# A 32-row rest of turned attention scores written by ScalarE and VectorE in place of transfers, and first-stage rows laid down by parity

## The chip, the cores and the metric

The kernel runs on one core of a Trainium2 chip. The metric is the device time of one execution in microseconds (us), the median of several runs. The engines are TensorE (PE, its weight loads PEld), VectorE (DVE), ScalarE (ACT), GpSimd (POOL) and SyncE (SP), which here only issues transfers.

## What is computed

One layer of a hybrid encoder block over 512 tokens of width 2048, in float32: a normalised and modulated input, one wide projection, two token mixers that read it (a dilated sliding-window attention with 16 heads of 64, and a gated linear attention with 4 heads), gates, an output projection, a residual and a final norm. The change lies in the first projection and in the attention, of which this is the core:

```python
for window, dilation in ((128, 1), (512, 4), (2048, 16)):
    s = einsum(q, keys at +-dilation*j) * E ** -0.5 + bias   # j up to 64, masked
    p = exp(s - max(s));  den = sum(p)
    o_p = (p / den) @ v                                      # and log-sum-exp lse_p
att = sum over patterns of softmax(lse)[p] * o_p
```

The kernel merges the three patterns into one softmax: a pair of positions that several patterns allow has the logarithm of their number added to its bias, and a pair that none allows is masked.

## The kernel before

**Numbers and products.** A float32 product is made of three products of two halves, `hi` (the rounded operand) and `lo` (what is left): hi*hi, lo*hi, hi*lo, lines 229, 230 and 231. So every operand is written twice, `hi` by ScalarE as a copy into a rounding type, and `lo` by VectorE as a subtraction. Weights come in by transfer as `raw_*` tiles and are split so at lines 493 (ScalarE) and 477 (VectorE).

**First stage.** Stage `a` (PSUM tiles `sta`, 16 steps `k`) multiplies the scaled input h by the attention's value weights; stage `b` (`stb`) makes the first queries and keys. `u_high` and `u_low` (lines 525 to 530) write h from x, 512 tokens a step. The values are wanted with even tokens ahead of odd ones. Before, h keeps the order of the tokens here, and stage `a` takes its stationary operand from h with `TOKENS`, four slices of 128 tokens with step two. Ahead of stage `b` h is written once more, in the order of the tokens.

**Attention.** It runs in the background of four projections, called units: `qk2`, `qk4`, `qk6` (which make the queries and keys of later heads) and `gk`. Each unit is 64 ticks of three matmuls of 512 columns; the attention of four heads is spread over it, as a list of items with places in the unit that come from `ATT_AT`. A head has four tiles `i` of 128 queries, and a tile has:

- `score(h, i)`: two matmuls of 416 columns into PSUM tile `s` (lines 817, 818); VectorE adds the bias from tile `g` and takes the least (825); ScalarE takes the exponential and its sum in place in tile `p` (829); VectorE the reciprocal (832); GpSimd scales the tile (836; ScalarE for the last two, 834).
- `turn(h, i)`, two scores later: three transposes of 128 columns into `t` (851), then ScalarE's `hi` (855) and VectorE's `lo` (856) into `pt`, one of two tiles that hold the turned scores of a pair of query tiles.
- `rest(h, e)`, with every second turn: 416 columns are three times 128 and 32 more. The 32 more of each of the two tiles of the pair are transposed into `r` (865), rounded and subtracted into a helper tile of 32 rows (867, 868), and sent by two transfers (871, on SP's queue) to their rows of `pt`: rows 96 to 127 for one half, rows 0 to 31 for the other.
- `values(h, e)`, once a pair: eight matmuls of 256 columns (880) over the four chunks of `pt` in the order 1, 2, 3, 0. Chunks 1 and 2 hold no row of the rest. Then 883 (ScalarE) and 887 (VectorE) write the head's output.

Beside each score VectorE does a piece of side work: token sums (1189 and after, 0.7 us) or bias sums of 1024 columns (959, 328).

**Order.** TensorE's order is the program's: per step x the list holds `score(x)`, `values` of the pair whose second tile was scored five steps ago, `turn(x - 2)`. The other engines' order is chosen by the scheduler of the language, which follows the dependences. PSUM has a ring of three buffers for `s`, `t` and `o`, and of five for the unit's four sums and `r`. SP issues all in order: weights, bias rows `g`, the rests, and the duplicates of queries (762, 765) and keys (774) across the two halves of the partitions, which `qk_evict` makes at the end of each unit.

Of the kernel before, what the change touches and what calls it, by code (L numbers as in the profile page):

```python
# [10 lines left out]
F32 = mybir.dt.float32  # L11
# [7 lines left out]
P = 128  # L19
# [90 lines left out]
ATT_AT = (0.17, 0.8, 0.04, 0.05, 0.02, 0.1)  # L110
# [80 lines left out]
def block_kernel(ctx: ExitStack, tc: tile.TileContext, a: dict):  # L191
# [332 lines left out]

    def u_high(k):
        act(h_hi[:, k, :], x_of(k), AF.Copy, scale=scale[:, k:k + 1])

    def u_low(k):
        stt(h_lo[:, k, :], x_of(k), scale[:, k:k + 1], h_hi[:, k, :].bitcast(F32),
            op0=ALU.mult, op1=ALU.subtract)  # L530
# [41 lines left out]
    def first_products(z, e):  # L572
# [3 lines left out]
        for i in range(4):  # L576
            j, t = 4 * z + i, TOKENS[i]
# [4 lines left out]
    def products(st, k, j):  # L582
# [3 lines left out]
        if st == "a":  # L586
            t, c = TOKENS[j % 4], slice(j // 4 * 512, j // 4 * 512 + 512)
# [164 lines left out]
    def qk_evict(p, psq, psk):  # L752
# [3 lines left out]
        for j in range(2):  # L756
            own = slice(64 * j, 64 * j + 64)
            oth = slice(64 - 64 * j, 128 - 64 * j)
            qh, ql = T2(f"qh{p}{j}", F32R), T2(f"ql{p}{j}", F32R)
# [6 lines left out]
            stacks[2 * p + j] = [qh, ql, None, own]  # L766
        for j in range(2):
            own = slice(64 * j, 64 * j + 64)
            oth = slice(64 - 64 * j, 128 - 64 * j)
            ks = key_tile(2 * p + j)  # L770
            src = psk[own].rearrange("p (c a) -> p a c", a=2)
            act(by_parity(ks, own), src, AF.Copy)
            tt(by_parity(ks, oth), src, by_parity(ks.bitcast(F32), own), op=ALU.subtract)
            nc.sync.dma_start(ks[:, 512:768].bitcast(F32), ks[:, 0:256].bitcast(F32))
            stacks[2 * p + j][2] = ks
# [19 lines left out]
    def attention(pairs):  # L795
# [11 lines left out]
        def score(h, i):  # L807
            def go():
# [11 lines left out]
                t = tile_[:, :NK]  # L820
# [12 lines left out]
                if (h, i) in ((15, 2), (15, 3)):  # L833
                    act(t, t, AF.Copy, scale=st[:, 2:3])
                else:
                    last["pool"] = nc.gpsimd.tensor_scalar(t, t, st[:, 2:3], 1.0, op0=ALU.mult, op1=ALU.mult).ins  # L836
                pr_[h, i] = t
            return go

        def turn(h, i):  # L840
            def go():
# [7 lines left out]
                first_ = 0 if half else 32  # L849
# [11 lines left out]
        def rest(h, e):  # L861

            pk = PJ(f"r{h}{e}")
            for half, c in ((0, 0), (1, 384)):
                nc.tensor.transpose(pk[:32, half * P:half * P + P], pr_.pop((h, 2 * e + half))[:, c:c + 32], ident)
            st = T2(f"r{h}{e}", F32R, 32)
            act(st[:, :256], pk[:32, :256], AF.Copy)
# [24 lines left out]
        for x in range(n + 5):  # L892
# [3 lines left out]
            if 0 <= v < n and v % 2 == 1:  # L896
                items.append(values(tiles[v][0], tiles[v][1] // 2))
# [872 lines left out]
```

## Time and profile before

| | us |
|---|---|
| median of 3 runs | 980.51 |
| lowest, highest | 980.43, 981.87 |
| the profiled execution | 982.41 |
| its span | 980.6 |
| TensorE busy | 918.0 (94%) |
| VectorE busy | 717.3 (73%) |
| ScalarE busy | 488.8 (50%) |
| GpSimd busy | 109.2 (11%) |
| attention stage | 205 to 515 |

A group's row reads: line, engine, operation, out<-in, shapes, xcount | busy us, mean ns of one | idle time of the engine before them and what ended it. A row of the wait list reads: who waited for what: us in total, times, longest. A row of a stretch reads: from:to length, busy us of PE, PEld, DVE, ACT and POOL with their counts, the clock granted to TensorE, the busy share of the 16 DMA engines, GB/s. A row of a tile's view has min/median/max ns. A row of the timeline reads: start, us, engine, line, operation, [idle before <- what ended it].

### The profile page before, as it was taken

How to read it: one execution, taken by the hardware profiler on the slowest of the kernel's cores; microseconds unless marked ns; L12 is line 12 of the kernel's file. 1: busy time of each engine (PE TensorE's matmuls, PEld its weight loads, DVE VectorE, ACT ScalarE, POOL GpSimd, SP SyncE). 2: the span in 40 equal slices, each digit the busy share in tenths (PEclk: the TensorE clock that was granted, in tenths of full speed). 3: DMA queues.
4: the chain of work that ended last, by engine and by line, in shares of the span. 5: the costliest groups of instructions: out<-in, count | busy, mean ns of one | idle time of the engine just before them, and what ended most of it. 6: DMA issues, size and time to landing. Idle time of an engine off the chain costs nothing.

```text
span 980.6 us, 12703 instructions
## 1 busy us (share of the span) xinstructions
PE 918.0 (94%) x4327; PEld 762.7 (78%) x4327; DVE 717.3 (73%) x1139; ACT 488.8 (50%) x836; POOL 109.2 (11%) x172
## 2 busy tenths in 40 slices
PE   8999999989697968969899999999999999999996
PEld 6888888867586857858687878888888888888885
DVE  8987999766565747746665866849587747898687
ACT  5553533644443534534455765437364427655555
POOL 0000000022121202212210001111102110000001
PEclk9999999999998989989999999999999999999999
DMA  9998596886867968886878886877877697896864
GB/s 356 403 414 340 199 349 225 236 212 173 202 196 195 237 181 226 219 213 180 215 217 270 246 273 236 264 245 234 241 242 233 202 311 254 294 329 213 285 239 164
DMA packets 76298, 244.20 MB, mean 249 GB/s; under 512 B 10213, under 2 KB 24837, under 8 KB 66633
## 3 DMA queue, kind: packets, MB, share of 16 engines
q1 hardware_dynamic: 69474, 201.08, 60.2%
q0 software_dynamic: 6464, 42.01, 18.0%
q8 instruction: 34, 0.56, 0.2%
q10 hardware_dynamic: 296, 0.30, 0.1%
q14 instruction: 30, 0.25, 0.1%
HBM read 225.44 MB, written 51.47 MB: 282 GB/s over the span
## 4 chain that ended last, share of the span: by engine, by line
PE 75%; DMA 13%; DVE 5%; ACT 3%; issue 2%; SPq 0%; DVEq 0%; POOL 0%; ACTq 0%; POOLq 0%
DMA pt<-r 11%; PE g L231 4%; PE g L230 3%; PE g L229 3%; PE stb L231 3%; PE stb L229 3%; PE stb L230 3%; PE sta L230 3%; PE sta L229 3%; PE sta L231 3%; PE ps_ag L229 3%; PE ps_ag L231 3%; PE ps_ag L230 3%; PE o L880 2%; PE ps_qk L229 2%; PE ps_qk L230 2%
## 5 line engine op out<-in xcount | busy, mean ns | idle before, releaser
L880 PE MATMUL o<-pt,vv 128*128 128x256 f32 x256 | 43.0, 302 | 47.9 <-DMA pt<-r 47.8
L880 PEld LDWEIGHTS o<-pt,vv 128*128 128x128 f32 x256 | 37.9, 199 | 54.4 <-DMA pt<-r 51.6
L328 DVE CUSTOM_DVE_ANT_0 cb<-cb,sb,c_bcond 128x2048 f32<-128x2048 f32 (+1 forms) x32 | 73.4, 2295 | 0.0
L836 POOL TENSOR_SCALAR p<-p,st 128x416 f32<-128x416 f32 x62 | 42.5, 686 | 248.4 <-DVE st L832 157.0
L829 ACT ACTIVATE p<-p,st 128x416 f32<-128x416 f32 x64 | 40.9, 639 | 54.0 <-DVE st L825 44.6
L825 DVE CUSTOM_DVE_ANT_0 p<-s,g 128x416 f32<-128x416 f32 (+1 forms) x64 | 30.6, 478 | 26.4 <-PE s L818 20.0
L887 DVE TENSOR_TENSOR cat<-o,oh 64x256 f32<-64x256 f32 x32 | 13.2, 413 | 46.9 <-ACT oh L883 46.8
L856 DVE TENSOR_TENSOR pt<-t,pt 128x384 fp32r<-128x384 f32 x64 | 35.4, 553 | 16.4 <-ACT pt L855 16.2
L883 ACT ACTIVATE oh<-o 64x256 f32<-64x256 f32 x32 | 12.2, 381 | 66.6 <-PE o L880 66.3
L855 ACT ACTIVATE pt<-t 128x384 fp32r<-128x384 f32 x64 | 31.0, 485 | 24.2 <-PE t L851 23.8
L429 POOL DMA_DIRECT2D T<-in_w_o x32 | 23.1, 722 | 168.3 <-ACT V2h L493 16.1
L851 PEld LDWEIGHTS t<-c_ident,p 128*128 128x128 f32 x192 | 25.6, 144 | 9.2 <-issue 0.6
L851 PE MATMUL t<-c_ident,p 128*128 128x128 f32 x192 | 32.5, 280 | 0.0
L817 PE MATMUL s<-ks,qh 128*128 128x416 f32 x64 | 22.7, 355 | 1.0 <-DMA ks<-ks 1.0
L818 PE MATMUL s<-ks,ql 128*128 128x416 f32 x64 | 22.8, 356 | 0.2 <-DMA ql<-ql 0.2
L328 DVE CUSTOM_DVE_ANT_0 rawg<-rawg,crow,c_bcond 128x1024 f32<-128x1024 f32 x16 | 20.3, 1279 | 2.6 <-issue 1.6
L1052 ACT ACTIVATE sq<-st,sc 128x256 f32<-128x256 f32 x24 | 12.2, 507 | 19.3 <-DVE st L1042 11.3
L328 DVE CUSTOM_DVE_ANT_0 rawg<-rawg,crow,gate 128x1024 f32<-128x1024 f32 x16 | 20.4, 1279 | 0.3 <-DMA rawg<-in_wg 0.3
L832 DVE RECIPROCAL st<-st 128x1 f32<-128x1 f32 x64 | 10.0, 156 | 12.4 <-ACT p L829 12.3
L429 POOL DMA_DIRECT2D T3V<-in_w_gv x8 | 5.6, 699 | 120.5 <-ACT qk21h L493 120.5
L1542 POOL TENSOR_SCALAR x<-x,rn 128x512 f32<-128x512 f32 x2 | 2.3, 1164 | 148.1 <-ACT rn L1531 143.7
L557 ACT ACTIVATE h_hi<-xt,shift 128x512 fp32r<-128x512 f32 x16 | 11.5, 719 | 12.9 <-DVE shift L328 12.9
(1660 smaller groups left out, 3151.3 us busy)
## 6 DMA issues: line engine op xcount, KB each, us to landing
cb<-in_wm SPq DMA_DIRECT2D x31, 1024.0 KB, 8.4
T<-in_w_o POOLq DMA_DIRECT2D x32, 512.0 KB, 6.1
rawg<-in_wg SPq DMA_DIRECT2D x32, 512.0 KB, 4.9
raw_O<-in_w_o SPq DMA_DIRECT2D x32, 512.0 KB, 4.4
raw_qk<-in_w_qk SPq DMA_DIRECT2D x24, 512.0 KB, 5.2
raw_O<-T SPq DMA_DIRECT2D x24, 512.0 KB, 4.9
rawb<-in_w_sb SPq DMA_DIRECT2D x16, 512.0 KB, 5.7
rawv<-in_wv SPq DMA_DIRECT2D x16, 512.0 KB, 4.6
```

The costliest lines, as they stand in the source:

```text
L229: mm(ps, lh, rh, start=first, stop=False, skip_group_check=more)
L230: mm(ps, ll, rh, start=False, stop=False, skip_group_check=more)
L231: mm(ps, lh, rl, start=False, stop=last, skip_group_check=more)
L328: return nc.vector.tensor_tensor_reduce(out=w, in0=w, in1=with_, op0=ALU.mult, op1=ALU.add, scale=1.0, scalar=init, accum_out=dst)
L429: move = nc.gpsimd.dma_start(dst, src, max_dma_last_dim=8192, **how).ins
L825: top = nc.vector.tensor_tensor_reduce(out=t[:, lo:hi], in0=ps[:, lo:hi], in1=gt[h][:, at:at + hi - lo], op0=ALU.add, op1=ALU.min, scale=1 ...
L829: act(t, t, AF.Exp, bias=st[:, 0:1], scale=-1.0, accum_out=st[:, 1:2])
L836: last["pool"] = nc.gpsimd.tensor_scalar(t, t, st[:, 2:3], 1.0, op0=ALU.mult, op1=ALU.mult).ins
L851: nc.tensor.transpose(pk[:, kt * P:kt * P + P], t[:, first_ + kt * P:first_ + kt * P + P], ident)
L855: act(hi, src, AF.Copy)
L856: tt(lo, src, hi.bitcast(F32), op=ALU.subtract)
L880: mm(po[:, :256], vv[h // 4][:, CHUNK_OF[e][c], h % 4, :], t[:, w, c, :], start=n_ == 0 and w == 0, stop=n_ == 3 and w == 1)
```

## The change

Three things are changed.

1. **The rest.** A query tile's 416 columns now lie at the end of the 512-column tile `p` for even tiles (columns 96 to 511) and at its start for odd ones. GpSimd scales an odd tile in two pieces: 384 columns in place, and the last 32 into columns 64 to 95 of the even tile beside it. So columns 64 to 127 of the even tile hold both rests of the pair. `rest` turns them with one transpose of 64 columns, and ScalarE and VectorE write the four pieces (two halves, `hi` and `lo`) straight into their rows of `pt`. The helper tile and the two transfers are gone.
2. **The order.** `values` comes three steps after the pair's second score in place of five, behind `turn`; the last of a unit is moved by 0.05 of the unit in place of 0.1, and the one ahead of it isn't moved.
3. **Parity.** `u_high` and `u_low` write h with even tokens in the first 256 columns and odd ones in the rest, reading x with step two, and stage `a` takes its weights as whole blocks of 128 columns. In `qk_evict` the keys of a head are now written and sent ahead of its queries, head by head.

```diff
-ATT_AT = (0.17, 0.8, 0.04, 0.05, 0.02, 0.1)
+ATT_AT = (0.17, 0.8, 0.04, 0.05, 0.05)
...
+    def halves_of(t):
+        return t.rearrange("p (a c) -> p a c", a=2)
+
+    def parities_of(t):
+        return t.rearrange("p (c a) -> p a c", a=2)
+
     def u_high(k):
-        act(h_hi[:, k, :], x_of(k), AF.Copy, scale=scale[:, k:k + 1])
+        act(halves_of(h_hi[:, k, :]), parities_of(x_of(k)), AF.Copy, scale=scale[:, k:k + 1])
...
-            t, c = TOKENS[j % 4], slice(j // 4 * 512, j // 4 * 512 + 512)
+            t, c = slice(j % 4 * P, j % 4 * P + P), slice(j // 4 * 512, j // 4 * 512 + 512)
...
-                t = tile_[:, :NK]
+                t = tile_[:, 0:NK] if i % 2 else tile_[:, 512 - NK:512]
...
-                if (h, i) in ((15, 2), (15, 3)):
-                    act(t, t, AF.Copy, scale=st[:, 2:3])
-                else:
-                    last["pool"] = nc.gpsimd.tensor_scalar(t, t, st[:, 2:3], 1.0, op0=ALU.mult, op1=ALU.mult).ins
-                pr_[h, i] = t
+                todo_ = [(t, t)]
+                if i % 2:
+                    todo_ = [(t[:, :384], t[:, :384]), (pr_[h, i - 1][:, 64:96], t[:, 384:416])]
+                for to, of in todo_:
+                    if (h, i) in ((15, 2), (15, 3)):
+                        act(to, of, AF.Copy, scale=st[:, 2:3])
+                    else:
+                        last["pool"] = nc.gpsimd.tensor_scalar(to, of, st[:, 2:3], 1.0, op0=ALU.mult, op1=ALU.mult).ins
+                pr_[h, i] = tile_
...
-            for half, c in ((0, 0), (1, 384)):
-                nc.tensor.transpose(pk[:32, half * P:half * P + P], pr_.pop((h, 2 * e + half))[:, c:c + 32], ident)
-            st = T2(f"r{h}{e}", F32R, 32)
-            act(st[:, :256], pk[:32, :256], AF.Copy)
-            tt(st[:, 256:], pk[:32, :256], st[:, :256].bitcast(F32), op=ALU.subtract)
-            st4 = st.bitcast(F32).rearrange("p (w half q) -> p w half q", w=2, half=2)
-            for half, rows, c in ((0, slice(96, 128), 3), (1, slice(0, 32), 0)):
-                nc.sync.dma_start(pts[e][rows, :, c, P * half:P * half + P].bitcast(F32), st4[:, :, half, :])
+            nc.tensor.transpose(pk[:64, :P], pr_.pop((h, 2 * e))[:, 64:128], ident)
+            del pr_[h, 2 * e + 1]
+            of = pk[0:32, :P], pk[32:64, :P]
+            to = [(pts[e][0:32, w, 0, P:2 * P], pts[e][96:128, w, 3, 0:P]) for w in range(2)]
+            for z in range(2):
+                act(to[0][z], of[z], AF.Copy)
+            for z in range(2):
+                tt(to[1][z], of[z], to[0][z].bitcast(F32), op=ALU.subtract)
...
-        for x in range(n + 5):
+        for x in range(n + 4):
             if x < n:
                 items.append(score(*tiles[x]))
-            v = x - 5
-            if 0 <= v < n and v % 2 == 1:
-                items.append(values(tiles[v][0], tiles[v][1] // 2))
             if 2 <= x <= n + 1:
                 items.append(turn(*tiles[x - 2]))
+            if x == n:
+                continue
+            for v in (x - 4, x - 3) if x == n + 1 else (x - 3,):
+                if 0 <= v < n and tiles[v][1] % 2 == 1:
+                    items.append(values(tiles[v][0], tiles[v][1] // 2))
...
-        at[-2] += move_next
         at[-1] += move_last
```

**TensorE, second head of unit `qk2`.** Names: `s` a score, `t` a turned tile, `r` a rest, `o` the values, `pt_...` the pair's turned scores, `ps_qk_...` the unit. Before, behind the third score of the head:

```order
L817 MATMUL s_1965<-ks_1545,qh_1549 128x416
L818 MATMUL s_1965<-ks_1545,ql_1550 128x416
L229 MATMUL ps_qk_3_1576<-h_hi,qk24h 128x512
L230 MATMUL ps_qk_3_1576<-h_hi,qk24l 128x512
L231 MATMUL ps_qk_3_1576<-h_lo,qk24h 128x512
L880 MATMUL o_1980<-pt_1677,vv_990 128x256 x8
L229 MATMUL ps_qk_3_1576<-h_hi,qk24h 128x512
L230 MATMUL ps_qk_3_1576<-h_hi,qk24l 128x512
L231 MATMUL ps_qk_3_1576<-h_lo,qk24h 128x512
L851 MATMUL t_1995<-c_ident,p_1882 128x128 x3
```

And in the changed kernel, behind a rest that stands four rows above the first of these:

```order
L819 MATMUL s_1977<-ks_1539,qh_1552 128x416
L820 MATMUL s_1977<-ks_1539,ql_1553 128x416
L229 MATMUL ps_qk_3_1576<-h_hi,qk24h 128x512
L230 MATMUL ps_qk_3_1576<-h_hi,qk24l 128x512
L231 MATMUL ps_qk_3_1576<-h_lo,qk24h 128x512
L857 MATMUL t_1992<-c_ident,p_1895 128x128 x3
L229 MATMUL ps_qk_0_1573<-h_hi,qk25h 128x512
L230 MATMUL ps_qk_0_1573<-h_hi,qk25l 128x512
L231 MATMUL ps_qk_0_1573<-h_lo,qk25h 128x512
L886 MATMUL o_2006<-pt_1745,vv_990 128x256 x8
```

The values that stood ahead of the turn are behind it, and they belong to the pair whose rest was turned last (`pt_1745`), where before they belonged to the pair ahead of that one (`pt_1677`).

**VectorE, head 4.** From the subtraction of a turned tile (`pt<-t`) to that of its pair's rest; `p<-s,g` is the bias step of another score, `S` a token sum, `st` a reciprocal. Before:

```order
L856 TENSOR_TENSOR pt_1677<-t_2480,pt_1677 128x3x128
L825 ISA p_2467,st_2468<-s_2464,g_2314,st_2468 128x160
L825 ISA st_2468 128x1
L1201 SCALAR_TENSOR_TENSOR S_2472<-S_2391,h_hi 128x512
L825 ISA p_2503,st_2504<-s_2500,g_2401 128x416
L825 ISA st_2504 128x1
L832 RECIPROCAL st_2468<-st_2468 128x1
L868 TENSOR_TENSOR r_2489<-r_2486,r_2489 32x256
```

And in the changed kernel:

```order
L862 TENSOR_TENSOR pt_1678<-t_2474,pt_1678 128x3x128
L827 ISA p_2460,st_2461<-s_2457,g_2306,st_2461 128x160
L827 ISA st_2461 128x1
L1208 SCALAR_TENSOR_TENSOR S_2465<-S_2383,h_hi 128x512
L877 TENSOR_TENSOR pt_1678<-r_2480,pt_1678 32x128
L834 RECIPROCAL st_2461<-st_2461 128x1
L827 ISA p_2495,st_2496<-s_2492,g_2393 128x416
L827 ISA st_2496 128x1
L877 TENSOR_TENSOR pt_1678<-r_2480,pt_1678 32x128
```

The same work stands between the turned tile and the rest; the rest's subtraction is two pieces now, and the second has the next score's bias step ahead of it.

**TensorE, end of unit `qk2`.** Before, from the second turned tile of the unit's last head (`p_2091`) to the third:

```order
L851 MATMUL t_2186<-c_ident,p_2091 128x128 x3
L865 MATMUL r_2192<-c_ident,p_2050 32x128
L865 MATMUL r_2192<-c_ident,p_2091 32x128
L229 MATMUL ps_qk_0_1573<-h_hi,qk27h 128x512
L230 MATMUL ps_qk_0_1573<-h_hi,qk27l 128x512
L231 MATMUL ps_qk_0_1573<-h_lo,qk27h 128x512
L880 MATMUL o_2208<-pt_1745,vv_990 128x256 x8
L229 MATMUL ps_qk_0_1573<-h_hi,qk27h 128x512
L230 MATMUL ps_qk_0_1573<-h_hi,qk27l 128x512
L231 MATMUL ps_qk_0_1573<-h_lo,qk27h 128x512
L851 MATMUL t_2224<-c_ident,p_2129 128x128 x3
```

And in the changed kernel, from the same turned tile to the last rest:

```order
L857 MATMUL t_2202<-c_ident,p_2108 128x128 x3
L870 MATMUL r_2208<-c_ident,p_2061 64x128
L229 MATMUL ps_qk_0_1573<-h_hi,qk27h 128x512
L230 MATMUL ps_qk_0_1573<-h_hi,qk27l 128x512
L231 MATMUL ps_qk_0_1573<-h_lo,qk27h 128x512
L857 MATMUL t_2218<-c_ident,p_2142 128x128 x3
L229 MATMUL ps_qk_1_1574<-h_hi,qk27h 128x512
L230 MATMUL ps_qk_1_1574<-h_hi,qk27l 128x512
L231 MATMUL ps_qk_1_1574<-h_lo,qk27h 128x512
L857 MATMUL t_2227<-c_ident,p_2186 128x128 x3
L870 MATMUL r_2233<-c_ident,p_2142 64x128
```

A value product that stood between the turned tiles is gone from here (it stands ahead of the last score now), and the last score, `p_2186`, is three matmuls ahead of `t_2202` where it was six.

More of the change, by code (lines that the diff above doesn't have):

```diff
@@ L765, in qk_evict @@
             nc.sync.dma_start(ql[oth].bitcast(F32), ql[own].bitcast(F32))
[L766 to L775, printed above, removed]
+            stacks[2 * p + j] = [qh, ql, ks, own]
     cat = [None] * 4
@@ L848, in go @@
                 pk = PA(f"t{h}{i}")
-                first_ = 0 if half else 32
+                first_ = 0 if half else 128
                 for kt in range(3):
```

11 lines of the change are left out of this document (8 added, 3 removed).

## The prediction

> **What bounds the kernel now.** I read the page first. TensorE carries the span: its busy digits are 9 nearly everywhere, and the dips lie in slices 9 to 20, the attention stage.
>
> ```profile
> PE 918.0 (94%) x4327; PEld 762.7 (78%) x4327; DVE 717.3 (73%) x1139; ACT 488.8 (50%) x836; POOL 109.2 (11%) x172
> PE   8999999989697968969899999999999999999996
> PEclk9999999999998989989999999999999999999999
> ```
>
> Next the list of waits, for TensorE alone. One entry is nearly all of it; the second row is the one other that bears on the change.
>
> ```profile
> PE o L880 <- DMA pt<-r: 47.8, 15, 8.9
> PE s L817 <- DMA ks<-ks: 1.0, 1, 1.0
> ```
>
> So 15 of the 32 value products stand still, up to 8.9 us, for the transfer that carries the 32-row rest of the turned scores. The tile view of the rest says why: ScalarE and VectorE need 0.36 and 0.40 us for it, the transfer behind them 2.4 to 12.7 us until it has landed.
>
> ```profile
> L867 ACT ACTIVATE r<-r x32: 355/358/363, 206.7 to 512.0; 32x256 fp32r<-32x256 f32 x32
> L868 DVE TENSOR_TENSOR r<-r,r x32: 392/404/407, 208.4 to 512.6; 32x256 fp32r<-32x256 f32 x32
> DMA to landing us min/median/max: 2.4/7.3/12.7
> ```
>
> Last the stretches: the whole attention stage, a piece of it in which TensorE never waits, and the piece around the first change of projection.
>
> ```profile
> 205.00:515.00 310.00, 262.09 (x1337) 220.73 (x1336) 196.31 (x496) 138.53 (x311) 64.14 (x97) 0.93 0.76 203
> 474.00:501.00 27.00, 27.00 (x148) 23.17 (x147) 21.33 (x58) 14.01 (x34) 7.33 (x13) 0.99 0.79 200
> 254.00:273.00 19.00, 10.08 (x48) 8.29 (x47) 8.38 (x15) 6.75 (x14) 2.73 (x4) 0.83 0.86 219
> ```
>
> The second row bears most of my trust: with the same side work, VectorE 79% busy and the transfers at 0.79, TensorE ran 27 us without a gap. The other engines can follow it when no rest holds it up.
>
> **The change, part by part.**
>
> *The waits.* The values no longer depend on a transfer, so 47.8 us go, if what takes its place is in time (below).
>
> *The clock.* A long wait costs a second time: the granted clock drops to 0.50 behind it. Seven stretches with 0.50 lie in the attention stage; the view of them (a small one, and the sum):
>
> ```profile
> 386.00:389.41 3.41, 3.41 (x13) 2.82 (x12) 0.75 (x3) 1.50 (x4) 0.61 (x1) 0.50 1.03 252
> sum 40.96, PE 27.54 PEld 22.61 DVE 7.48 ACT 9.59 POOL 2.07; mean PE 3.93 PEld 3.23 DVE 1.07 ACT 1.37 POOL 0.30
> ```
>
> TensorE was busy 27.5 us in them at half speed, work of 13.8 us at full clock: 13.8 us go with the waits. What wait is long enough? Two places of the timeline:
>
> ```profile
> 256.87 0.74 PE L880 MATMUL o<-pt,vv 128*128 128x256 f32 x4 [1.75 <-DMA pt<-r]
> 385.70 1.00 PE L880 MATMUL o<-pt,vv 128*128 128x256 f32 x4 [2.79 <-DMA pt<-r]
> 386.50 0.63 PE L229 MATMUL ps_qk<-h_hi,qk63h 128*128 128x512 f32 x1
> 257.00:261.00 4.00, 4.00 (x24) 3.39 (x25) 1.75 (x4) 2.17 (x6) 0.00 (x0) 1.00 0.88 190
> ```
>
> Behind 1.75 us the clock stays at 1.00, behind 2.79 us it is 0.50. So what is left of a wait costs only itself while it stays under some 2 us. The Trainium skill, "TensorE: Matmul & The Clock Gate", section "What's actually happening", gives the idle time that throttles as a window of about 3.4 us; by that the wait of 2.79 us, and another of its kind, would have cost no clock, and this term would be half of two such stretches, 3.4 us, smaller. The rows disagree, since 3.41 us at 0.50 follow the 2.79 us, and I keep 13.8.
>
> *The rest's transposes.* 64 of 32 columns become 32 of 64 columns. From the timeline, start to start:
>
> ```profile
> 222.91 0.49 PE L851 MATMUL t<-c_ident,p 128*128 128x128 f32 x3
> 223.24 0.38 PE L865 MATMUL r<-c_ident,p 128*32 128x128 f32 x2
> 223.38 0.48 PE L229 MATMUL ps_qk<-h_hi,qk23h 128*128 128x512 f32 x1
> ...
> 224.16 0.35 PE L817 MATMUL s<-ks,qh 128*128 128x416 f32 x1
> ...
> 224.53 0.40 PE L229 MATMUL ps_qk<-h_hi,qk23h 128*128 128x512 f32 x1
> 224.76 0.39 PE L230 MATMUL ps_qk<-h_hi,qk23l 128*128 128x512 f32 x1
> ...
> 225.22 1.11 PE L880 MATMUL o<-pt,vv 128*128 128x256 f32 x8
> ```
>
> Two cost 0.14 us, one of 128 columns 0.11 (0.33 for three). One of 64 columns lies between 0.07 and 0.11; I take 0.08, so 0.06 x 32 = 1.9 us less (1.0 to 2.2).
>
> *The first stage.* Its weight loads step over every second row today; the change lays the rows together. Stage one against a product whose rows lie together:
>
> ```profile
> L229 PEld LDWEIGHTS sta<-sa1hi,h_hi x8: 193/193/193, 16.2 to 21.4; 128*128 128x128 f32 x8
> L229 PE MATMUL sta<-sa1hi,h_hi x8: 393/394/397, 16.4 to 21.6; 128*128 128x512 f32 x8
> L229 PEld LDWEIGHTS ps_gv_P<-V0h,h_hi x4: 187/187/187, 515.8 to 517.8; 128*128 128x128 f32 x4
> L229 PE MATMUL ps_gv_P<-V0h,h_hi x4: 389/389/389, 516.0 to 518.1; 128*128 128x512 f32 x4
> ```
>
> Load and product are 5 to 6 ns shorter each; over 384 matmuls that TensorE issues without a gap this is 1.9 to 2.3 us. A little may be lost early, where the low parts of h come just in time; I take 1.8 (0 to 2.3). That ScalarE and VectorE now read x with a step of two I cost at nothing: it is as many elements in as many instructions, on engines that are busy 50% and 73% of the span; without that room, 0.05 us more on each of the 32 would be 1.6 us. The Trainium skill, "SBUF — State Buffer", section "Door 1: The DMA port swizzle", lets an fp32 reader step within 16 bytes for free; by that this term would be 0. The rows show 6 ns, so I keep it.
>
> *What is added, and where.* Per value product ScalarE gets two copies of 32x128 for one of 32x256, VectorE two subtractions for one, GpSimd a second scaling of 128x32. ScalarE: 358 less (485 - 358) = 0.23 us each; VectorE: 404 less (553 - 404) = 0.26 us each, from these rows and those above:
>
> ```profile
> L855 ACT ACTIVATE pt<-t 128x384 fp32r<-128x384 f32 x64 | 31.0, 485 | 24.2 <-PE t L851 23.8
> L856 DVE TENSOR_TENSOR pt<-t,pt 128x384 fp32r<-128x384 f32 x64 | 35.4, 553 | 16.4 <-ACT pt L855 16.2
> L825 DVE CUSTOM_DVE_ANT_0 p<-s,g 128x416 f32<-128x416 f32 x30 | 17.6, 585 | 11.1 <-PE s L818 10.1
> L825 DVE CUSTOM_DVE_ANT_0 p<-s,g,st 128x160 f32<-128x160 f32 x16 | 6.1, 382 | 0.4
> L825 DVE DVE_READ_ACCUMULATOR2_ANT st<- 128x1 f32 x94 | 7.7, 82 | 0.1
> L328 DVE CUSTOM_DVE_ANT_0 rawv<-rawv,shb,vbias 128x1024 f32<-128x1024 f32 x8 | 10.3, 1293 | 0.0
> L832 DVE RECIPROCAL st<-st 128x1 f32<-128x1 f32 x64 | 10.0, 156 | 12.4 <-ACT p L829 12.3
> L829 ACT ACTIVATE p<-p,st 128x416 f32<-128x416 f32 x64 | 40.9, 639 | 54.0 <-DVE st L825 44.6
> L829 ACT ACTIVATION_READ_ACCUMULATOR p<-p,st 128x1 f32 x63 | 11.8, 187 | 0.0
> L836 POOL TENSOR_SCALAR p<-p,st 128x416 f32<-128x416 f32 x62 | 42.5, 686 | 248.4 <-DVE st L832 157.0
> 203.97 0.69 DVE L1189 TENSOR_TENSOR S3e<-h_lo 128x512 f32<-128x512 f32 x1
> 205.04 1.22 DVE L477 TENSOR_TENSOR qk24l<-raw_qk,qk24h 128x1024 fp32r<-128x1024 f32 x1 [0.38 <-ACT qk24h L493]
> ```
>
> VectorE's total grows by 32 x 0.12 = 4 us, ScalarE's by 3. The small scaling has no row; between 0.05 (0.69 by size) and 0.69 us I take 0.2, and GpSimd waits most of the time.
>
> Now the cover. The changed order puts the value product much nearer to its rest: between them on TensorE usually stand 12 matmuls of 512 columns (0.23), one score pair (0.37) and three transposes (0.33), 3.5 us; the first four of its eight products don't read the rest (0.14 each, 0.5 us). So the last write has 4.0 us, and about 3.3 in the one place of eight with three matmuls fewer. It needs: ScalarE's copy of the turned tile, about 0.3 us past the rest's transpose, and then VectorE's queue. The long form is in the rows at head 4 in the section on the change: 0.55 + 0.38 + 0.08 + 0.69 + 0.26 + 0.16 + 0.59 + 0.08 + 0.26 = 3.05 us, done at 3.4. At the 3.3 us places VectorE's piece is half as long. Four of 32 have one of the 1.29 us sums in it and come to 3.3 to 4.0. So the cover mostly holds, with little to spare; I charge 1.0 us in all. If it were gone, each late microsecond costs 32 times itself.
>
> *The end of each projection.* Here the new order takes something away. The last score of a projection used to have six more matmuls and a value product (1.4 and 1.1 us) ahead of its own turning than now: what is left is nine matmuls, two turned tiles and one rest, 2.07 + 0.7 = 2.8 us. Its chain is 0.45 (256 columns, an estimate between the rows of 160 and 416) + 0.08 + 0.38 + 0.08 on VectorE, 0.64 + 0.19 on ScalarE, 0.16 on VectorE and 0.63 on GpSimd (384 of 416 columns) = 2.6 us, with four hand-overs of about 0.1 each 3.0; and a weight split of 1.22 us stands ahead of the reciprocal on VectorE, which makes up to 3.4. TensorE waits about 0.5 us at three of these ends; in the fourth ScalarE does the scaling and must also turn that tile and empty the projection (0.49 and some 0.6) before the last rest gets its PSUM buffer, so 0.5 and 1.2: 3.2 together. It is short enough to leave the clock alone.
>
> *The keys.* The duplicates of a new projection's queries and keys still go by transfers. From the end of the product that they are made of to the first score TensorE has 45 matmuls, two value products, two turned tiles and a rest, 13.3 us; the two copies take some 1.3 (512 columns by the slopes above), and the longest landing above was 12.7. So most land in time, and I charge 1.3 us; that the keys and queries of a head are now written one after the other moves each by a copy or two, and is inside that. The waits of 1.2 us at the very first scores stay. 64 transfers leave SP's queue, which helps what stands behind them.
>
> *Sum, against the profiled execution* (982.4 us; its span is 980.6, and the median of the runs shown, 980.5, lies 1.9 below it): 982.4 - 47.8 - 13.8 - 1.9 - 1.8 + 1.0 + 3.2 + 1.3 = 922.6; as a median 1.9 less, 920.7, say **921 us**.
>
> **Rivals.** *VectorE takes the transfer's place.* If one more 1.22 us split or 1.29 us sum stands ahead in the 24 ordinary places, each is about 1 us late: 24 us, no clock lost, 945 us. For it: VectorE goes from 196 us of 310 to 200 of some 248, 81%, and 3.4 of 4.0 us are used already. Against: 79% in the gapless row. 8%.
>
> *The transfers stay the bound at the changes of projection.* Their share is 0.76 over 310 us; the same work in 248 us would be 0.95, less the rests' own. The keys could then land 5 us late three times, with half of 3.4 us of clock each: 20 us, 941. For it: 0.86 at 254 to 273. Against: weights are fetched several groups ahead. 8%.
>
> *Slower.* The gain is 65 us over 32 products, 2.0 us each. If the rests' last write came 4.0 + 2.0 = 6.0 us after the transpose at all of them, nothing would be left, and past that, with the clock down behind each third wait (half of 3.4 us), it ends near 997. It needs VectorE's queue nearly twice as long as its rows. 2%.
>
> *The change removes a cause and not the wait*: the values might have waited for something else that the landing hid. The rows name VectorE and ScalarE done within a few us, so 2%, near 977 with the two small terms alone.
>
> **Numbers.** My forecast has 80%: 921, by its own unknowns 914 (no new wait at all) to 933. The range 913 to 944 takes in most of the two middle rivals. A measurement of this kernel tells 0.2%, 2 us, from no change. Faster 0.96, same 0.02, slower 0.02.
>
> **What would show it.** The wait of the value products on a transfer is gone from TensorE's list, and the clock digits of the attention stage read 9 throughout. TensorE's new waits are at the turned tiles, for GpSimd, under 1 us each. The weight loads of the first stage read 187. I am wrong if value products wait for VectorE or ScalarE by more than 10 us in all, or if the key copies are the longest wait.

## The result, and the profile after

The changed kernel takes 920.42 us (median of 4 runs, 918.27 to 920.61) where the one before took 980.6 beside it. The ratio on record is 0.9379, a little below that of the two medians (0.9386); its 95% interval is 0.9362 to 0.9395. The forecast was 921. The span of the profiled execution goes from 980.6 to 918.7 us.

The page of the changed kernel, for the rows shown of before:

```profile
PE 897.0 (98%) x4295; PEld 746.2 (81%) x4295; DVE 723.6 (79%) x1171; ACT 497.4 (54%) x869; POOL 117.6 (13%) x203
PE   8999999999999999999999999999999999999996
PEclk9999999999999999999999999999999999999998
```

The dips in TensorE's slices 9 to 20 and the eights of the clock there are gone. VectorE and ScalarE are busy 6 and 9 us longer than before, in a span that is 62 us shorter.

The list of waits, TensorE alone (two rows of the start, of 1.5 and 0.4 us, are left out):

```profile
PE s L819 <- DMA qh<-qh: 3.6, 2, 2.0
PE r L870 <- DVE pt L877: 2.3, 3, 0.8
PE sta L586 <- ACT h_hi L532: 2.0, 1, 2.0
PE r L870 <- ACT gkt L1267: 1.5, 1, 1.5
PE kv L1042 <- DVE gv L1390: 0.5, 1, 0.5
PE t L857 <- POOL p L842: 0.3, 2, 0.2
```

No value product stands in it. New are the waits at the rest's transpose, those of the first scores of a unit for the copies of the queries, and, at 0.3 us, those of turned tiles for GpSimd. The whole stage as one stretch, 250 us in place of 310, with the clock at 1.00:

```profile
205.00:455.00 250.00, 241.88 (x1291) 204.60 (x1290) 200.93 (x521) 145.95 (x337) 70.95 (x125) 1.00 0.92 247
```

What the rest costs now, from the tile view of `r`, and GpSimd's small scaling from the groups by shape:

```profile
L875 ACT ACTIVATE pt<-r x64: 249/266/269, 202.9 to 450.9; 32x128 fp32r<-32x128 f32 x64
L877 DVE TENSOR_TENSOR pt<-r,pt x64: 267/282/290, 204.7 to 451.7; 32x128 fp32r<-32x128 f32 x64
L842 POOL TENSOR_SCALAR p<-p,st 128x32 f32<-128x32 f32 x31 | 8.8, 283 | 0.0
```

0.27, 0.28 and 0.28 us, where 0.23, 0.26 and 0.2 were estimated.

**Where the 61.9 us come from.** For each PSUM tile the trace gives TensorE's time from the start of a matmul to the start of the next (without the wait) and its waits. All tiles that differ by more than 0.2 us:

| tile | waits before | waits after | running before | running after |
|---|---|---|---|---|
| `o`, values | 47.9 | 0.2 | 37.6 | 31.1 |
| `ps_qk`, `ps_gk`, the units | 0 | 0 | 192.1 | 183.8 |
| `r`, rests | 0 | 3.8 | 4.4 | 0.9 |
| `s`, scores | 1.2 | 3.6 | 24.9 | 25.0 |
| `t`, turned tiles | 0 | 0.5 | 19.1 | 19.2 |
| `sta`, first stage | 1.9 | 2.6 | 90.5 | 88.3 |
| `kv` | 1.3 | 0.5 | 9.1 | 9.1 |
| `pc`, at the very start | 0 | 0 | 3.5 | 2.8 |

Waits fall by 41.0 us and running time by 21.0. As many products run in the units and the values as before, in 14.8 us less. Most of it is the clock: in the seven stretches at 0.50 these products took 25.4 us, and half of that, 12.7 us, was lost. The other 2 us fit a cost behind the waits at full clock: seven value products with a wait among their eight matmuls took 1.25 us on average, the wait itself left out, where most without a wait took 0.95.

### The profile page after: what moved, and what is told of

Read it like the earlier page. It is cut to its first block, busy times and chain, and to the rows that moved or that the text cites. A ratio compares the mean times of both kernels' runs of the same rounds, so it can differ in the third digit from the quotient of the medians.

```text
span 918.7 us, 12571 instructions
## 1 busy us (share of the span) xinstructions
PE 897.0 (98%) x4295; PEld 746.2 (81%) x4295; DVE 723.6 (79%) x1171; ACT 497.4 (54%) x869; POOL 117.6 (13%) x203
## 4 chain that ended last, share of the span: by engine, by line
PE 81%; DMA 7%; DVE 6%; ACT 3%; issue 2%; SPq 0%; POOL 0%; DVEq 0%; ACTq 0%; POOLq 0%
PE g L231 4%; PE g L230 4%; PE g L229 4%; PE ps_qk L229 4%; PE ps_qk L231 4%; PE ps_qk L230 4%; PE stb L231 3%; PE stb L229 3%; PE stb L230 3%; PE ps_ag L229 3%; PE ps_ag L231 3%; PE ps_ag L230 3%; PE sta L230 3%; PE sta L231 2%; PE sta L229 2%; PE ps_gg L230 2%
## 5 line engine op out<-in xcount | busy, mean ns | idle before, releaser
L842 POOL TENSOR_SCALAR p<-p,st 128x416 f32<-128x416 f32 (+2 forms) x93 | 51.2, 555 | 181.8 <-DVE st L834 130.1
L886 PEld LDWEIGHTS o<-pt,vv 128*128 128x128 f32 x256 | 35.0, 189 | 3.5 <-DVE pt L877 0.6
L886 PE MATMUL o<-pt,vv 128*128 128x256 f32 x256 | 36.3, 283 | 0.2
L889 ACT ACTIVATE oh<-o 64x256 f32<-64x256 f32 x32 | 12.2, 382 | 13.9 <-PE o L886 12.9
L429 POOL DMA_DIRECT2D T<-T x16 | 8.4, 525 | 80.3 <-ACT V18h L493 9.7
L563 ACT ACTIVATE h_hi<-xt,shift 128x512 fp32r<-128x512 f32 x16 | 11.5, 719 | 12.9 <-DVE shift L328 12.9
L877 DVE TENSOR_TENSOR pt<-r,pt 32x128 fp32r<-32x128 f32 x64 | 17.9, 279 | 0.7
```

Of the source, the lines that this page charges most:

```text
L429: move = nc.gpsimd.dma_start(dst, src, max_dma_last_dim=8192, **how).ins
L842: last["pool"] = nc.gpsimd.tensor_scalar(to, of, st[:, 2:3], 1.0, op0=ALU.mult, op1=ALU.mult).ins
L886: mm(po[:, :256], vv[h // 4][:, CHUNK_OF[e][c], h % 4, :], t[:, w, c, :], start=n_ == 0 and w == 0, stop=n_ == 3 and w == 1)
```

## Experiments

Times are compared by their ratio to the kernel before on the same chip, and where a few microseconds matter, by the waits of the profiled execution.

### 1. The transfers with the new order

The kernel before with only the new list of items and their places (change 2, shown in part); the rest still goes by transfers.

```diff
-            v = x - 5
...
             if 2 <= x <= n + 1:
                 items.append(turn(*tiles[x - 2]))
...
+            for v in (x - 4, x - 3) if x == n + 1 else (x - 3,):
```

> The kernel before with only the new order of the items; the rest still goes by transfers. Theory (the landing is what the values wait for): the fifth product stands 4.1 us behind the rest's transpose, and the rest needs about 2 us on ScalarE and VectorE and 7.3 us to land, so nearly all 32 value products wait, 4 to 6 us each, 130 to 190 us in all against 47.8, and the clock falls more often: 1080 to 1200 us. Rival (the order alone shortens something): 980 or less. The waits come in many lengths here, so they also show behind which length the clock reads 0.50: by the rows of before between 1.75 and 2.8 us, by the rule of 3.4 us not below that.

Measured: 1067.39 us, a ratio of 1.0858 (1.083 to 1.0886). One row of TensorE's waits says it:

```profile
PE o L880 <- DMA pt<-r: 108.7, 27, 10.0
```

27 of 32 value products wait for the landing. The direction is the theory's; the size is below it, 4.0 us a wait, at the lower end of what was expected, and five pairs without one. (A TensorE that stands still gives the transfers more time, which may be the reason; no run tests it.) So the landing was what the values waited for, and the new order without the direct writes costs some 85 us, by the ratio and against the 982.58 us of the kernel before on this chip.

### 2. The direct rest with the old order

The changed kernel with the list of items and `ATT_AT` of before, the edit of experiment 1 the other way round.

> The changed kernel with the order of before: values five steps behind the second score, ahead of the turn, and the old places at the end of a unit. Theory (the direct writes bring the gain, the new order costs a little): the waits for the transfer and the clock stay away, and so do the 4.3 us of waits at the unit ends (3.8 at rests, 0.5 at turned tiles) and the 0.2 us of the values: 920.4 - 4.5 = 916, between 914 and 918. Rival (the new order is part of the gain: values that come late hold the two pt tiles and the PSUM buffers of the turned tiles): new waits at t or s of 5 us or more, 925 or above.

Measured: 920.4 us, 0.9359 (0.9342 to 0.9376), the same as the changed kernel within the intervals. So the direct rest, with the 2 us of change 3 that is still in (experiment 6), brings the whole gain, and the new order brings nothing beside it. Neither theory was right about the rest of it. The waits at the rests did go, but a new one came, and what it waited for is seen by following it back in the timeline (start, length, engine, line; in brackets the idle time and what ended it):

```profile
255.70 0.27 ACT L948 ACTIVATE shiftt<-pshift 16x128 f32<-16x128 f32 x1
265.33 0.38 ACT L889 ACTIVATE oh<-o 64x256 f32<-64x256 f32 x1 [9.37 <-DMA srow<-shiftt]
265.75 0.42 DVE L893 TENSOR_TENSOR cat<-o,oh 64x256 f32<-64x256 f32 x1 [8.81 <-ACT oh L889]
266.20 0.59 DVE L827 CUSTOM_DVE_ANT_0 p<-s,g 128x416 f32<-128x416 f32 x1
268.14 1.96 POOL L842 TENSOR_SCALAR p<-p,st 128x416 f32<-128x416 f32 x1 [20.36 <-PE ps_qk L231]
270.16 0.90 PE L857 MATMUL t<-c_ident,p 128*128 128x128 f32 x3 [2.54 <-POOL p L842]
```

Read from the bottom: the turned tile waits 2.54 us for GpSimd, GpSimd for a score whose bias VectorE added late (its row names a product of TensorE, but the reciprocal that it scales by is ready at 267.99, 0.15 us ahead of it), VectorE stood 8.81 us behind ScalarE's copy of the last values, and that copy 9.37 us for a transfer that reads `shiftt`, a small tile of the coming side work. `shiftt` and `oh` are given the same one buffer. In the changed kernel the last values of this unit are ahead of `shiftt`, and there is no such wait. GpSimd's scaling itself takes 1.96 us here, where its mean in this kernel is 0.79; these 1.2 us are part of the wait too, and why they came was not tried.

### 3. The old order with a buffer of its own for that tile

Experiment 2 with one line changed:

```diff
-        t = sm.tile([KT, P], F32, tag="oh", name="shiftt", bufs=1)
+        t = T2("shiftt")[:KT, :P]
```

> The kernel direct_rest_old_order with one line changed: the small tile shiftt, which shares one buffer with the copies oh of the value products, gets another buffer. In direct_rest_old_order the last values of unit qk2 come behind shiftt, so their copy waits 9.4 us on ScalarE for the transfer that reads shiftt, VectorE stands 8.8 us behind that copy, the bias of the next scores is late, and a turned tile waits 2.5 us and halves the clock for 3.4 us. Theory: that chain is all that the old order costs; both go, 2.5 + 1.7 us, span 919.9 - 4.2 = 915.7, within 1.5 us (waits for the copies of queries differ by that much between runs). Rival (the scores there are late for another reason): the wait at the turned tile stays above 1 us, span above 918.

Measured: 917.02 us, 0.9327 (0.9304 to 0.935), the lowest ratio here, below the interval of the changed kernel; span 915.6. ScalarE's copy now waits 0.74 us, for TensorE itself (the timeline), and no wait at a turned tile, a rest or a value product is left in TensorE's list; what remains of the attention stage there are two rows:

```profile
257.25 0.38 ACT L889 ACTIVATE oh<-o 64x256 f32<-64x256 f32 x1 [0.74 <-PE o L886]
```

```profile
PE s L819 <- DMA qh<-qh: 2.7, 3, 1.6
PE s L820 <- DMA ql<-ql: 0.3, 1, 0.3
```

So the shared buffer was what the old order cost at its turned tiles, and the new order costs 4.3 us at the unit ends that the old one does not have. That the span came out at the expected 915.7 is in part luck: this execution has two stretches at 0.50 ahead of its end, 3.41 us each, one in the first stage and one behind a wait of 1.58 us for the queries.

### 4. What the rests at the unit ends wait for

In the changed kernel, the end of unit `qk2`:

```profile
244.28 0.27 PE L870 MATMUL r<-c_ident,p 128*64 128x128 f32 x1
245.65 0.53 ACT L875 ACTIVATE pt<-r 32x128 fp32r<-32x128 f32 x2
246.26 0.27 DVE L877 TENSOR_TENSOR pt<-r,pt 32x128 fp32r<-32x128 f32 x1
246.37 0.55 PE L857 MATMUL t<-c_ident,p 128*128 128x128 f32 x3
247.30 0.29 DVE L877 TENSOR_TENSOR pt<-r,pt 32x128 fp32r<-32x128 f32 x1
247.73 0.27 PE L870 MATMUL r<-c_ident,p 128*64 128x128 f32 x1 [0.81 <-DVE pt L877]
```

The last tile is turned without a wait. The last rest could follow it at 246.92, but its PSUM buffer holds the rest before it until VectorE's second subtraction, at 247.59: the four sums of the unit and `r` share five buffers. Two edits were made. The first gives all rests of a unit one tile, the two pairs of a head two places in it:

```diff
-            pk = PJ(f"r{h}{e}")
+            if not held_r:
+                held_r.append(PJ(f"r{h}"))
+            pk = held_r[0][:, 2 * P * e:2 * P * e + P]
```

> The changed kernel with one PSUM tile for all rests of a unit, the two pairs of a head in two places of it, in place of a new tile for each rest. In the changed kernel the last rest of a unit waits 0.8, 0.8 and 0.8 us until VectorE has read the rest before it, and 1.5 us until ScalarE has emptied a sum of the projection. Theory (these are waits for a PSUM buffer, not for the scores): all four go, 3.8 us, 916 to 917.5. Rival (the scores are late there, so the wait only moves): the turned tile or the value product behind them waits instead, time within 1 us of 920.

Measured: 919.8 us, 0.9398 (0.937 to 0.9425), no change that can be told. The wait is as long as before:

```profile
PE r L872 <- DVE pt L879: 3.7, 4, 1.4
```

This tells nothing on the theory: here the last rest waits for VectorE to read the rest before it, which lies in another place of the same tile. So two places of one bank did not do as two buffers. The second edit needs no buffer: the last rest of a unit goes into the quarter of its turned tile's bank that is free, ahead of that tile's copies.

```diff
+                if (h, i) == (heads[-1], 3):
+                    nc.tensor.transpose(pk[:64, 3 * P:], pr_[h, 2][:, 64:128], ident)
                 hi = pt[:, 0, half:half + 3, P * half:P * half + P]
...
+            if (h, e) == (heads[-1], 1):
+                pk = pk[:, 3 * P:]
+            else:
+                pk = PJ(f"r{h}{e}")
+                nc.tensor.transpose(pk[:64, :P], pr_[h, 2 * e][:, 64:128], ident)
```

> The changed kernel with the last rest of each unit transposed into the free quarter of the PSUM bank of its turned tile, ahead of the copies out of that bank; it needs no buffer of its own. rests_in_one_bank did not answer, since a transpose into a bank waits for the readers of the whole bank. Theory (the four waits of 3.8 us are for a PSUM buffer): they go, and 0.1 to 0.2 us is added at each turned tile for GpSimd's second piece: 918.7 - 3.3 = 915.4 us of span, within 1.5. Rival (the rest's input is late too): the wait moves to the rest's transpose for GpSimd or to the value products, 3 us or more, span 918 to 919.

Measured: 917.47 us, 0.9342 (0.9319 to 0.9364); its profiled execution is its slowest, span 918.0, and the expected span was missed. What it waits for in the attention stage:

```profile
PE s L819 <- DMA qh<-qh: 3.9, 2, 2.2
PE t L857 <- POOL p L842: 0.3, 2, 0.2
```

No wait at a rest is left, and none took its place behind it: value products wait 0.2 us in all, as before. So these waits were for a PSUM buffer. The span fell by 0.7 us in place of 3.8. Of the missing 3.1 us, 1.7 are the clock, which a wait of 2.2 us for the queries halved once in this execution, and 0.5 are longer waits for the queries; the remainder is spread and was not traced.

### 5. How much cover the value product has

Per pair, the trace of the changed kernel gives the last write of the rest and the fifth product of the values, both from the rest's transpose. The fifth product stands 4.08 us behind it at 20 of 32 pairs, 3.38 at four and 5.4 to 6.1 at the eight of the unit ends; the last write is done after 1.5 to 4.4 us, median 3.25. What is left over is -0.3 to 4.1 us, median 1.1. To see when this gives way, the two subtractions are repeated, with the same result:

```diff
-            for z in range(2):
+            for z in [0, 1] * 3:
                 tt(to[1][z], of[z], to[0][z].bitcast(F32), op=ALU.subtract)
```

> The changed kernel with each rest's two subtractions made three times (the same values again): the last write comes 4 x 0.28 = 1.12 us later on VectorE, the output is the same. In the changed kernel's trace the fifth product of a pair stands 4.08 us behind the rest's transpose (3.38 at four places, more at the unit ends), and the last write is done 1.5 to 4.4 us behind it; what is left over is -0.3 to 4.1 us, median 1.1. Theory (each pair has its own small cover): 16 of 32 pairs get late, 12 us in all by the sum over the pairs of what 1.12 us overshoots, a little more for VectorE's longer queue: 12 to 17 us, 932 to 937, as waits of value products for VectorE. Rival (VectorE has 50 idle us of 250 in the stage and absorbs 36 us more): 0 to 3 us, below 924.

> The same with five rounds of the two subtractions, the last write 8 x 0.28 = 2.24 us later, 72 us more on VectorE in all. Theory: 27 of 32 pairs late, 36 us by the same sum, and since VectorE then has 273 of some 290 us in the stage, its queue adds 5 to 20 us: 41 to 56 us, 961 to 976, no clock lost as long as the single waits stay under about 1.8 us in a window of 3.41 us. Rival (idle time absorbs it): 72 - 50 = 22 us at most, 942.

Measured: 963.24 us, 0.9836 (0.9805 to 0.9868), and 1032.67 us, 1.0535 (1.0505 to 1.0565). Both theories were far too low. The rows of one pair of the first, VectorE behind the transpose, show why (the `L870` row is the transpose; the reciprocal, the bias of the next score and the tile turned next are left out where "..." stands):

```profile
279.46 0.27 PE L870 MATMUL r<-c_ident,p 128*64 128x128 f32 x1
...
281.71 0.27 DVE L877 TENSOR_TENSOR pt<-r,pt 32x128 fp32r<-32x128 f32 x1
...
282.83 0.60 DVE L877 TENSOR_TENSOR pt<-r,pt 32x128 fp32r<-32x128 f32 x2
...
283.36 0.67 DVE L1211 TENSOR_TENSOR S<-S,h_lo 128x512 f32<-128x512 f32 x1
284.06 0.59 DVE L877 TENSOR_TENSOR pt<-r,pt 32x128 fp32r<-32x128 f32 x2
...
285.20 0.29 DVE L877 TENSOR_TENSOR pt<-r,pt 32x128 fp32r<-32x128 f32 x1
285.55 0.61 PE L886 MATMUL o<-pt,vv 128*128 128x256 f32 x3 [1.72 <-DVE pt L877]
```

The repeats do not stay together: the scheduler puts a token sum, a reciprocal and another tile's subtraction between them. The last write is done 6.0 us behind the transpose here and 5.28 at the median, 2.0 later than in the changed kernel and not 1.12. With that delay the picture of one small cover a pair holds: 24 pairs overshoot, by 35.5 us in all, and these are the waits, with three stretches of half clock beside them in the stage:

```profile
PE o L886 <- DVE pt L877: 30.2, 22, 2.2
PE r L870 <- DVE pt L877: 7.5, 3, 2.5
```

VectorE is idle 48 us of 250 in this stage, and no absorption is to be seen: 36 us of subtractions were added, and the time rose by 43. So its idle time lies elsewhere in its queue. With twice the repeats the last write comes 6.66 us behind the transpose at the median, the value products wait 64.6 us, and 21 stretches of half clock lie in the stage; that takes back the whole gain and 52 us more.

### 6. The small terms

Weight loads with step two and h in the order of the tokens, as before (all of change 3 but `qk_evict` undone; one of its lines):

```diff
-            t, c = slice(j % 4 * P, j % 4 * P + P), slice(j // 4 * 512, j // 4 * 512 + 512)
+            t, c = TOKENS[j % 4], slice(j // 4 * 512, j // 4 * 512 + 512)
```

> The changed kernel with h of the first stage in the order of the tokens and weight loads with step two, as before. Theory (a load with step two costs 5 to 6 ns on TensorE): the products of the first stage take 2.2 us more, the 0.5 us wait for the first low parts of h goes, so 1.7 us more, 921.5 to 922.5. Rival (a step of two is free, the difference of stage a came from elsewhere): within 0.4 us of 920.4.

Measured: 922.4 us (921.87 to 923.42), 0.9383 (0.937 to 0.9395); the time is the theory's, but the interval takes in the changed kernel, so it alone decides nothing. The rows of stage `a` do: in this kernel, and then in the changed one,

```profile
L229 PEld LDWEIGHTS sta<-sa1hi,h_hi x8: 193/193/195, 16.4 to 22.2; 128*128 128x128 f32 x8
L229 PE MATMUL sta<-sa1hi,h_hi x8: 392/394/503, 16.4 to 22.4; 128*128 128x512 f32 x8
```

```profile
L229 PEld LDWEIGHTS sta<-sa1hi,h_hi x8: 187/187/188, 15.6 to 21.1; 128*128 128x128 f32 x8
L229 PE MATMUL sta<-sa1hi,h_hi x8: 388/389/389, 15.8 to 21.3; 128*128 128x512 f32 x8
```

6 ns a load again, and the 384 products run 90.8 us against 88.3. That the wait for the first low parts would go was wrong (0.8 us, against 0.4).

Queries ahead of keys in `qk_evict`, as before:

> The changed kernel with the old order inside qk_evict, queries of both heads ahead of keys. In the changed kernel two first scores of a unit wait 3.6 us for the copies of the queries, in the one before none did. Theory A (the copies land late because four bias rows and a weight tile are ahead of them in the queues, whichever is sent first): the wait stays between 2.5 and 5 us, for queries or keys, and the time within 1 us of 920.4. Theory B (the order of keys and queries makes it): the wait falls below 1 us, the time to 917 to 918.

Measured: 921.29 us (917.51 to 924.58), 0.937 (0.9348 to 0.9392), the same. Its profile has 1.6 us of waits at scores where the changed kernel's has 3.6. But the kernel with the rows by step, whose `qk_evict` is the changed one, has 1.1, and over all ten profiles with a direct rest these waits go from 0.1 to 4.8 us. So the difference cannot be put down to the order, theory B is not shown, and theory A was wrong to expect a steady wait. Why a copy lands late in one execution and not in another stays open.

Each rest's transpose issued twice:

```diff
+            for _ in range(2):
+                nc.tensor.transpose(pk[:64, :P], pr_[h, 2 * e][:, 64:128], ident)
```

> The changed kernel with each rest's transpose of 64 columns issued twice into the same place: 32 more on TensorE. Theory from the changed kernel's trace (start to start it takes 0.03 us): start to start the 32 add 0.9 to 1.2 us in the rests' rows. Rival (0.08 us each, as forecast): 2.6 us. A transpose of 128 columns would be 3.5 us.

Measured: 922.0 us (one run). The timeline of one rest in the changed kernel, and then with two:

```profile
209.36 0.49 PE L857 MATMUL t<-c_ident,p 128*128 128x128 f32 x3
209.69 0.27 PE L870 MATMUL r<-c_ident,p 128*64 128x128 f32 x1
209.72 0.48 PE L229 MATMUL ps_qk<-h_hi,qk23h 128*128 128x512 f32 x1
210.03 0.39 PE L230 MATMUL ps_qk<-h_hi,qk23l 128*128 128x512 f32 x1
```

```profile
211.11 0.38 PE L871 MATMUL r<-c_ident,p 128*64 128x128 f32 x2
211.25 0.49 PE L229 MATMUL ps_qk<-h_hi,qk23h 128*128 128x512 f32 x1
211.57 0.40 PE L230 MATMUL ps_qk<-h_hi,qk23l 128*128 128x512 f32 x1
```

From the rest to the second product behind it are 0.34 us with one and 0.46 with two. Over all 32, the rests' running time goes from 0.93 to 4.39 us: 0.108 us for one more transpose, that of one of 128 columns, and the 4.4 us that two of 32 columns took before. Both theories were too low; the sum is that of the expectation's last sentence, 3.5 us for transposes of 128 columns.

## Why the prediction was right, and where it was not

| step | forecast | measured |
|---|---|---|
| waits for the transfer | -47.8 | -47.9 |
| clock (running time of units and values) | -13.8 | -14.8 |
| the rest's transposes | -1.9 | -3.4 |
| first stage | -1.8 | -1.5 |
| values late | +1.0 | +0.2 |
| ends of units | +3.2 | +4.3 |
| keys and queries | +1.3 | +2.5 |
| `kv`, `pc`, not forecast | 0 | -1.5 |
| sum | -59.8 | -62.1 |

(The measured sum differs from 61.9 by rounding and the tiles left out.)

**The waits and the clock** were the gain, by the mechanism of the forecast: experiment 1 keeps the transfers and has 108.7 us of waits, experiment 2 keeps the old order and has none at the values. The clock's term is less exact than it looks: the forecast's 13.8 us had 1.1 us at scores and turned tiles, whose running time did not fall, and the 14.8 hold 2 us behind waits at full clock, which the forecast did not have. Its reading that a wait under some 2 us is harmless rested on one of 1.75 us, and that one is no proof (last section).

**The cover** was sized well: 4.08 and 3.38 us against 4.0 and 3.3, and 3.4 for what the forecast took for a long chain, which is nearer to the median, 3.25. That its worst cases reach 4.4 costs next to nothing, as only the overshoot of single pairs counts. The rival that VectorE takes the transfer's place was near: in experiment 5 a last write that comes 2.0 us later at the median costs 43 us, and one that comes 3.4 us later makes the kernel slower than before; the forecast had put that point at 2.6 us (6.0 against 3.4), and the runs have it between the two.

**The ends of the units** came out near the right size, for a reason that is half wrong. The forecast had turned tiles waiting for GpSimd, 0.5 us at three ends. They wait 0.2 us or less there; the rests behind them wait 0.8 us at each, for the PSUM buffer that the rest before holds. Only at the fourth end, where the forecast did name such a buffer (1.7 us with its turned tile), is it nearly as forecast: 1.5 us for ScalarE's `gkt`. Experiment 4 shows that it is the buffer. (In the kernel with doubled transposes only one of the four ends waits, 1.2 us; why was not traced.)

**The rest's transposes** were mis-sized. The step read 0.14 us for two, start of the first to start of the next product. But the product behind a rest is held up as well (0.48 us in its row, where the following ones have 0.39), the same 0.08 behind one rest as behind two, so that the difference of one transpose is a whole one, 0.11 us. Its columns make no difference: the matmul's own row reads 128x128 for 32 and for 64 of them.

**The first stage** gave 2.2 us of running time, as worked out from the rows (1.9 to 2.3); 0.7 us more of waits at its start took part of it back. The other kernels with a direct rest have 1.5 to 2.9 us there, and the one before 1.9, so that the 0.7 are not shown to be the change's. Reading x with step two, and writing it in halves, was put at nothing: ScalarE's 16 copies take 750 ns in place of 709, 0.7 us in all, VectorE's subtractions 747 in place of 744.

**The copies at the start of a unit** hide less well than forecast, and it is the queries that are late and not the keys. As they vary by more than that from execution to execution, the 1.2 us between forecast and measurement mean little. The rival in which the transfers stay the bound had their busy share right (0.92 in the stage, 0.95 forecast), but in the changed kernel no copy held TensorE for more than 2.0 us, where it had 5. `pc` varies too, by less (2.4 to 3.5 us). The wait at `kv`, far behind the attention, is 0.7 us or less in all profiles with a direct rest and 1.3 and 2.2 in the two with transfers; why was not tried.

**What was added** was somewhat underestimated and lies beside TensorE: ScalarE has 5.2 us more at the rests (16.6 against 11.4), VectorE 5.0 (17.9 against 12.9), where 3 and 4 were expected.

**The signs.** Three came: no value product waits for a transfer, the clock digits of the stage read 9, the first stage's loads 187. One did not: the new waits are not at the turned tiles but at the rests (0.8 us at three ends, 1.5 at the fourth) and at first scores. And one sign of being wrong was near: the copies of the queries, if not of the keys, make the longest wait behind the first stage, 2.0 us.

## What to carry to other kernels

A small piece of a tile that goes by a transfer costs its landing: here a median of 7.3 us from the issue alone, where with a few short operations in its place the last write is done 3.3 us behind the transpose. When the distance between producer and consumer is cut at the same time, look for the next thing that is shared, here a PSUM buffer at the unit ends; keeping the longer distance and mending one shared buffer was worth another 3 us by the medians, 5 by the ratios. And size a cover pair by pair: an engine that was idle for a fifth of the stage did not absorb what was put into its queue at the wrong place.

## What the runs showed of the hardware

The clock does not follow the length of a wait alone. In every trace with several stretches at 0.50 they begin on a grid of 3.413 us (22 of them in the kernel with the rest 2 us later), and a fall goes with how much of one such window TensorE stood idle. Three waits are examples. One of 2.79 us in the kernel before lies inside one window, the first row here (the wait's row, and that of the window behind it, stand in the prediction); two are of the kernel of experiment 1, the shorter one inside a window and the longer one across an edge. The windows give from:to and length, TensorE's busy time, ..., and the clock in the third number from the end. The window of the kernel before, the timeline of the kernel of experiment 1, and then its windows:

```profile
382.59:386.00 3.41, 0.61 (x5) 0.41 (x4) 1.84 (x4) 0.00 (x0) 0.00 (x0) 1.00 0.78 149
```

```profile
334.23 0.96 PE L880 MATMUL o<-pt,vv 128*128 128x256 f32 x4 [1.78 <-DMA pt<-r]
544.51 0.74 PE L880 MATMUL o<-pt,vv 128*128 128x256 f32 x4 [2.80 <-DMA pt<-r]
```

```profile
331.15:334.56 3.41, 1.63 (x10) 1.29 (x9) 1.11 (x3) 0.76 (x3) 1.07 (x2) 1.00 0.76 209
334.56:337.97 3.41, 3.41 (x12) 2.88 (x11) 1.16 (x4) 0.38 (x1) 0.00 (x0) 0.50 0.32 118
539.36:542.77 3.41, 2.35 (x14) 1.87 (x12) 2.40 (x7) 1.11 (x3) 1.04 (x2) 1.00 0.81 251
542.77:546.19 3.42, 1.68 (x10) 1.55 (x11) 0.42 (x1) 0.38 (x1) 0.00 (x0) 1.00 0.60 229
546.19:549.60 3.41, 3.41 (x19) 2.89 (x18) 2.65 (x10) 2.31 (x5) 0.61 (x1) 1.00 0.23 53
```

The wait of 1.78 us, inside one window, is followed by 0.50. The one of 2.80 us, split into 1.06 and 1.74, costs no clock, where the one of 2.79 us inside a window did. As 1.78 and 1.74 are too near to each other to show a bound, the count of all windows must: over all traces, the end of each execution left out, the 50 windows at full clock with 1.93 us or more of idle time are all followed by half clock, of the 22 with 1.5 to 1.9 us two are (the other holds 1.58 us, in experiment 3), and of the 54 with 1.0 to 1.5 us none. Fourteen waits of 1.95 to 2.80 us that an edge divides, no part longer than 1.89 us, cost no clock. So in these traces a wait was safe by itself up to 1.5 us and mostly up to 1.9; what made the two exceptions stays open. Whether several short waits in one window count together is not shown: each fall in the attention has a single wait of 1.58 us or more in its window. The forecast's "some 2 us" was partly luck: an edge divides its wait of 1.75 us into 1.18 and 0.57. The Trainium skill, "TensorE: Matmul & The Clock Gate", section "What's actually happening", calls the window free-running and 3413 ns long, and the traces agree with both; it lets the clock fall after an idle window, and here 1.93 us, a little more than half a window, was always enough.
